# Encoder trunk: start of the FFNs, convolution module, last transposes and GLA gates of a four-layer kernel rearranged

## The chip, the cores and the metric

The kernel runs on one core of a Trainium2 chip. The metric is the device time of one execution in microseconds (us), as the median of several runs. TensorE (PE) multiplies matrices, VectorE (DVE), ScalarE (ACT) and GpSimd (POOL) work elementwise, and the queue of SyncE (SP) issues the transfers of weights.

## The reference

Four layers on `x` of 1 x 256 x 1024 (float32). Each layer is a half-step SwiGLU FFN (inner width 2816), a token mixer, and another half-step FFN, each with an RMSNorm ahead and a residual add. The mixers are, in order, dilated window attention, a Conformer convolution module, Fourier mixing and bidirectional gated linear attention (GLA). The change touches the FFN and the second and the fourth mixer:

```python
def _swiglu(h, w1, w3, w2):
    return (jax.nn.silu(h @ w1) * (h @ w3)) @ w2

def _conv_module(u, ...):
    z = u @ w_pw1 + b_pw1
    a, gate = jnp.split(z, 2, axis=-1)
    z = a * jax.nn.sigmoid(gate)
    z = lax.conv_general_dilated(z, w_dw, ...) + b_dw      # 31 taps, depthwise
    zf = (z - mu) * lax.rsqrt(var + EPS) * ln_g + ln_b     # mu, var over the 1024 features
    return jax.nn.silu(zf) @ w_pw2 + b_pw2

def _gla_direction(q, k, v, log_a, include_diag):
    # S_t = diag(a_t) S_{t-1} + k_t v_t^T, o_t = q_t S_t, in chunks of 64 tokens
...
# GLA mixer, 4 heads, q and k 512 wide, v and r 1024 wide
def log_decay(d):                                          # d: forward, backward
    z = (u @ w_a1[d]) @ w_a2[d] + b_a[d]                   # rank 16
    return jax.nn.log_sigmoid(z) / GLA_TAU
o = o_fwd + o_bwd
o = rmsnorm over each head of o, times norm_g, times silu(r)
return o @ w_o
```

## The kernel before, in words

Activations lie transposed, 128 features on the partitions by 256 tokens, in pieces `x0` to `x3`. A float32 product is made of pairs: each operand is split into a high part (rounded to fp32r) and a low part (the rest), and `mm3` issues three matmuls, high by high, high by low, low by high. All of them go through `mm` (L81). The FFN's `wide` puts two of the three into one matmul of 512 columns, so there a product is one of 256 and one of 512 columns.

Weights come in blocks of 1 MB, 128 x 2048, over SP's queue into 4 buffers `raw`. `split_block` turns a block into a pair `w`: ACT writes the high part (L167), DVE subtracts (L170). There are 4 buffers `w`; `take` hands the next pair to the matmuls in the order of a plan, `done` counts a buffer as free, and `pump(n)` emits up to `n` splits for buffers counted free. On each engine the instructions run in the order in which the code emits them, so a split stands on ACT and DVE exactly where its `pump` is in the code. PSUM has 8 banks, A0 to A3 and B0 to B3. One half collects up-projections (`ab` hands its banks out in turn) and the other half the down-projections (`dbank`); the halves change roles from stage to stage.

- **FFN** (`ffn`): blocks `w1`, `w3` in turn into banks PA, PB. ACT copies one half of the result to a tile `sl` or `br` (`parts`, L466), DVE adds the other (`add`, L471), so the banks come free. The stage begins with four k-steps of both blocks, then `pump(1)`, then the rest, since the last x come late from the stage before. `stats(True)` sums squares on PE and gives R by a Newton iteration on DVE (L410, then L367 to L373), in steps that `ffn` emits among its own. The product with the silu is split into `g` (ACT L635, DVE L636). In the last FFN, `fin_transpose` (L84) transposes the finished first half of the output on PE while the second half is multiplied.
- **Convolution** (`pre1`, `mix1`): 24 products `wd` of 128 x 256 (a mask times the taps, L671) are made on GpSimd during the FFN ahead. After the taps, the mean and variance are summed on PE, and each piece `zc` is multiplied with the inverse deviation (DVE L876), goes through Silu (ACT L880), and is split (ACT L635, DVE L636). `pump(1)` follows behind pieces 1 and 2.
- **GLA** (`pre3`, `mix3`): `qkproj` makes q and k, `qkevac` moves them out of PSUM (DVE L1223). The gate's low rank part `t1` (17 rows for each direction, one of them ones for the bias) is multiplied by `wa2` in four float32 matmuls (`gate_a`), set between steps of `qkproj(2)`. Then `vproj(i)` and `rproj(i)` (8 steps of 6 matmuls of 256 columns each) stand among the stages of the heads: `decays`, `states`, `scores`, `out` (L1403 sums squares, L1409 makes o) and `trans`, which transposes o on PE.

Of the kernel before, what the change touches and what calls it, by code (L numbers as in the profile page):

```python
# [15 lines left out]
D = 1024  # L16
# [3 lines left out]
EPS = 1e-6  # L20
NP = NG // 2
NR = 4
NW = 4
GLA_ORDER = [("gv", 0), ("gr", 0), ("gv", 1), ("gr", 1), ("gv", 2), ("gr", 2), ("gv", 3), ("gr", 3)]
# [14 lines left out]
class Enc:  # L39
    def __init__(self, ctx, tc, a, stages):  # L40
# [11 lines left out]
        self.lower, self.nab, self.held = 0, 3, []  # L52
# [9 lines left out]
    def ab(self):  # L62

        self.nab = (self.nab + 1) % 4
        while self.nab in self.held:
            self.nab = (self.nab + 1) % 4
        return self.bank(self.lower, self.nab)
# [5 lines left out]
    def bank(self, half, j):  # L73
        return self.banks[half][j]
# [25 lines left out]
    def plan(self):  # L100
# [7 lines left out]
        for st in self.stages:  # L108
# [26 lines left out]
            elif st[1] == 2:  # L135
                add(("cs",), a["c_cs"], 2)
                for j in range(4):
                    add(("wf", j), a["fnet_w"][j], 2)
            elif st[1] == 3:
                for i in range(4):  # L140
                    add(("gqk", i), a["gla_w_in"][i], 8)
                for n, i in GLA_ORDER:
                    add((n, i), a["gla_w_in"][{"gv": 4, "gr": 8}[n] + i], 8)
                for j in range(4):
                    add(("go", j), a["gla_w_o"][j], 2)
# [256 lines left out]
    def stats(self, row=False, scale=1.0):  # L402

        if row:
# [5 lines left out]
            nc.vector.tensor_scalar(y, p, 1.0 / D, EPS, ALU.mult, ALU.add)  # L410
            return self.newton_rsqrt(y, self.R, [128, 256], "nR", 1, 3)
# [31 lines left out]
    def ffn(self, l, s):  # L443
# [44 lines left out]
        for n, ks in enumerate(cuts):  # L488
            if n == len(cuts) - 1:
                if not first:  # L490
                    self.pump(1)
# [16 lines left out]
        steps.pop(0)()  # L508
        br0 = parts(PB, "br")
# [5 lines left out]
        for i in range(1, NG):  # L515
# [8 lines left out]
            if i == 4 and pre:  # L524
                self.pre = pre()
# [37 lines left out]
        for p in range(NP):  # L563
            self.pump(1)
            if p < 2 and self.nstage >= len(self.stages):
                self.fin_transpose(p)
# [79 lines left out]
    def open_pre(self):  # L646
# [3 lines left out]
        if n < len(self.stages) and self.stages[n][0] == "mix" and hasattr(self, f"pre{self.stages[n][1]}"):  # L650
            self.prest = ExitStack()
            self.prepool = self.prest.enter_context(self.tc.tile_pool(name=self.name("pre"), bufs=1))
            return getattr(self, f"pre{self.stages[n][1]}")
# [3 lines left out]
    def pre1(self):  # L657
# [9 lines left out]
        wd = {}  # L667
        for j in (0, 2, 3):
            wd[j] = self.sb(P, [128, 8, 8, 32], F32, f"wd{j}")
            for n in range(8):  # L670
                nc.gpsimd.tensor_tensor(wd[j][:, n], m32.unsqueeze(1).to_broadcast([128, 8, 32]),  # L671
                                        wt[:, 8 * j + n].unsqueeze(2).to_broadcast([128, 8, 32]), ALU.mult)
        return wc, wd

    def mix1(self):
# [102 lines left out]
        def factor():  # L778
            steps = self.stats(True)
            self.pump(1)  # L780
# [56 lines left out]
        self.sqrt_table()  # L837
        nc.vector.tensor_tensor(sqs[:, 0], sqs[:, 0], sqs[:, 1], ALU.add)
        for c in range(2):
            nc.vector.scalar_tensor_tensor(zc[3][:, c], dwp[3][:, 256 * c:256 * c + 256], self.col(("bdw", 6 + c)), m0,  # L840
                                           ALU.add, ALU.subtract)
            nc.scalar.activation(s2[:, c], zc[3][:, c], AF.Square)
        nc.vector.tensor_tensor(sqs[:, 0], sqs[:, 0], sqs[:, 2], ALU.add)
# [26 lines left out]
        nn = self.sb(ev, [128, 2, 2, 2, 256], F32R, "zs", 3)  # L870
        for i in range(4):
            gp = self.pair(self.hp, [128, 2, 256], f"x{i}") if i < 2 else nn[:, i - 2]
            hi, lo = gp[:, 0], gp[:, 1]
            for c in range(2):
                z = zc[i][:, c]
                nc.vector.tensor_tensor(z, z, rp, ALU.mult)  # L876
                gb = dict(scale=self.col(("lng", 2 * i + c)), bias=self.col(("lnb", 2 * i + c)))
                if i == 0:
                    nc.scalar.activation(hi[:, c], z, AF.Silu, **gb)
# [3 lines left out]
            if i:  # L883
                for c in range(2):
                    self.split(zc[i][:, c], gp[:, :, c])
            g.append(gp)
            if i in (1, 2):
                self.pump(1)
# [262 lines left out]
    def pre3(self):  # L1151

        nc, P = self.nc, self.prepool
        raw = lambda shape: self.sb(self.ev, shape, F32, "craw", 2)

        wa = raw([128, 8, 64])
        nc.gpsimd.memset(wa, 0.0)
        for d in range(2):
            nc.gpsimd.dma_start(wa[:, :, 32 * d:32 * d + 16],
                                self.a["gla_w_a1"][0, d].rearrange("(k p) n -> p k n", p=128))  # L1160
        traw = raw([128, 2, 256])
        nc.gpsimd.dma_start(traw, self.a["c_tri"])
        was = self.pair(P, [128, 8, 64], "was")
        self.split(wa, was)
# [3 lines left out]
        nc.gpsimd.dma_start(lraw, self.a["c_tril"])  # L1168
        mraw = raw([128, 2, 256])
        nc.gpsimd.dma_start(mraw, self.a["c_mask"])  # L1170
        lst = self.sb(P, [128, 2, 128], F32R, "lst")
        nc.scalar.activation(lst, lraw, AF.Copy)
        mask = self.sb(P, [128, 2, 256], mybir.dt.uint8, "mask")
        nc.vector.tensor_copy(mask, mraw)
        wa2 = self.sb(P, [64, 512], F32, "wa2")
        for d in range(2):
            nc.gpsimd.dma_start(wa2[32 * d:32 * d + 16, :], self.a["gla_w_a2"][0, d])
            nc.gpsimd.dma_start(wa2[32 * d + 16:32 * d + 17, :], self.a["gla_b_a"][0, d:d + 1, :])
        return was, wa2, tri, lst, mask

    def mix3(self):
# [6 lines left out]
        bkn = [0]  # L1188

        def bank(hold=False):  # L1190

            bkn[0] += 1
            if self.D4 is None and bkn[0] % 2:
                return self.dbank(bkn[0] // 2 % 4)
            p = self.ab()
            if hold:
                self.held = [self.nab]
            return p
# [7 lines left out]
        vt = [self.sb(ev, [128, 1024], F32, f"gv{t}") for t in range(2)]  # L1206
# [26 lines left out]
        for k in range(8):  # L1233
            self.mm3(pa[0:64, 0:256], was[:, :, k], self.xk(k), start=k == 0, stop=k == 7)
        self.bcast()
        t1 = T([64, 256])
        nc.gpsimd.memset(t1, 1.0)
        for d in range(2):
            pr = slice(32 * d, 32 * d + 16)
            nc.vector.tensor_tensor(t1[pr], pa[pr, 0:256], self.R[pr], ALU.mult)  # L1240
        qkevac(0, p0)
        qkevac(1, p1)

# [6 lines left out]
        def gate_a(d, t):  # L1250
            pr = slice(32 * d, 32 * d + 17)
            p = bank()
            self.mm(p, t1[pr, 128 * t:128 * t + 128], wa2[pr, :], start=True, stop=True)
# [23 lines left out]
        def vproj(i):  # L1277

            def step(k, s):
                if k == 0:  # L1280
# [291 lines left out]
def lay(a, perm=True):  # L1572


    o = {}
# [65 lines left out]
```

## Time and profile before

| | |
|---|---|
| runs, us | 1929.97, 1930.38, 1933.54 (median 1930.38) |
| the profiled execution, us | 1932.82 |
| its span, us | 1930.7 |
| PE busy | 1902.6 us (99%) in 12128 matmuls |
| PE loading weights | 1674.7 us (87%) |
| DVE busy | 1396.7 us (72%) |
| ACT busy | 994.8 us (52%) |
| POOL busy | 34.9 us (2%) |
| DMA | 338.08 MB, mean 175 GB/s |

Busy time of an engine is its share of the span; a stall of PE is told in brackets behind a row of the timeline, with the instruction that ended it.

### The profile page before, as it was taken

Reading aid. Unit: us, or ns where it says so; the run is one execution under the profiler, and the core shown is the slowest. Engines: PE = TensorE matmul, PEld = TensorE weight load, DVE = VectorE, ACT = ScalarE, POOL = GpSimd, SP = SyncE. Lnnn points to the kernel's source line nnn. Section 1 sums busy time; section 2 is a strip of 40 time slices with the busy share of each in tenths; the row PEclk is TensorE's granted clock in tenths of the full one; section 3 lists DMA queues with packets and bytes.
Section 4 is the critical chain, followed back from the end, with each engine's and each line's share of the span. In section 5 each row is a group of like instructions: output and inputs, shape, how many; then the busy total and the mean of one; then the engine's idle time right before and its main releaser. Section 6 shows DMA issues by size and latency. Waiting matters only on the chain.

```text
span 1930.7 us, 28911 instructions
## 1 busy us (share of the span) xinstructions
PE 1902.6 (99%) x12128; PEld 1674.7 (87%) x12128; DVE 1396.7 (72%) x1850; ACT 994.8 (52%) x1267; POOL 34.9 (2%) x55
## 2 busy tenths in 40 slices
PE   8999999999999999899999999999999999999998
PEld 6888899888888898788888889988888888998886
DVE  7776567877697767787768776787777766668774
ACT  6554444654455544565545554555445445756452
POOL 0000000000040000000000000000000000000000
PEclk9999999999999999899999999999999999999999
DMA  7655533465445543246545554365546553335550
GB/s 265 221 193 195 189 130 132 155 219 193 175 173 210 188 170 137 85 159 220 192 175 198 195 178 172 131 218 191 182 168 221 199 193 115 129 129 196 198 195 22
DMA packets 48643, 338.08 MB, mean 175 GB/s; under 512 B 5568, under 2 KB 5744, under 8 KB 8192
## 3 DMA queue, kind: packets, MB, share of 16 engines
q1 hardware_dynamic: 47952, 335.11, 48.8%
q8 instruction: 95, 1.56, 0.3%
q0 software_dynamic: 560, 1.12, 0.2%
q14 instruction: 36, 0.29, 0.0%
HBM read 335.16 MB, written 1.05 MB: 174 GB/s over the span
## 4 chain that ended last, share of the span: by engine, by line
PE 92%; DVE 5%; ACT 2%; issue 1%; DMA 0%; SPq 0%; DVEq 0%; ACTq 0%
PE B L81 50%; PE A L81 41%; DVE w L170 1%; ACT w L167 1%; DVE zc L765 1%; PE A L84 0%; DMA h<-in_x_dram 0%; ACT zc L880 0%; ACT x L302 0%; PE B L84 0%; DVE h L279 0%; DVE acc L355 0%; DVE x L304 0%; DVE sl L474 0%; DVE nRu L372 0%
## 5 line engine op out<-in xcount | busy, mean ns | idle before, releaser
L170 DVE TENSOR_TENSOR w<-raw,w 128x2048 fp32r<-128x2048 f32 x315 | 720.2, 2293 | 288.6 <-ACT w L167 288.2
L167 ACT ACTIVATE w<-raw 128x2048 fp32r<-128x2048 f32 x315 | 598.9, 1909 | 113.5 <-PE A L81 47.4
L81 PE MATMUL B<-x,w 128*128 128x256 f32 (+1 forms) x3968 | 643.7, 322 | 1.3 <-DVE sl L471 1.1
L81 PEld LDWEIGHTS B<-x,w 128*128 128x128 f32 x3968 | 571.3, 190 | 71.5 <-issue 5.5
L81 PE MATMUL A<-x,w 128*128 128x256 f32 x3008 | 521.5, 334 | 10.3 <-DVE w L636 6.8
L81 PEld LDWEIGHTS A<-x,w 128*128 128x128 f32 x3008 | 455.8, 190 | 73.1 <-DVE w L636 6.8
L81 PE MATMUL B<-g,w 128*128 128x256 f32 (+1 forms) x1408 | 251.2, 336 | 0.7 <-DVE w L170 0.6
L81 PE MATMUL A<-g,w 128*128 128x256 f32 (+1 forms) x1408 | 250.3, 336 | 0.0
L81 PEld LDWEIGHTS B<-g,w 128*128 128x128 f32 x1408 | 216.5, 187 | 32.7 <-issue 0.9
L81 PEld LDWEIGHTS A<-g,w 128*128 128x128 f32 x1408 | 216.6, 187 | 31.5
L635 ACT ACTIVATE g<-br 128x512 fp32r<-128x512 f32 x88 | 55.6, 632 | 253.6 <-DVE br L480 253.6
L474 DVE TENSOR_TENSOR sl<-sl,R 128x512 f32<-128x512 f32 x176 | 121.7, 695 | 2.5
L636 DVE TENSOR_TENSOR g<-br,g 128x512 fp32r<-128x512 f32 x88 | 61.1, 695 | 61.5 <-ACT g L635 61.5
L302 ACT ACTIVATE x<-h,cols 128x256 fp32r<-128x256 f32 x88 | 39.9, 501 | 67.8 <-DVE h L279 49.0
L466 ACT ACTIVATE br<-B 128x256 f32<-128x256 f32 x88 | 30.2, 385 | 75.0 <-PE B L81 75.0
L477 ACT ACTIVATE sl<-sl 128x512 f32<-128x512 f32 x88 | 55.0, 628 | 26.6 <-DVE sl L474 26.5
L466 ACT ACTIVATE br<-A 128x256 f32<-128x256 f32 x88 | 30.1, 384 | 70.4 <-PE A L81 70.4
L480 DVE TENSOR_TENSOR br<-sl,br 128x512 f32<-128x512 f32 x88 | 60.6, 689 | 0.5
L81 PE MATMUL B<-w,x 128*128 128x256 f32 (+2 forms) x360 | 60.8, 327 | 0.0
L81 PEld LDWEIGHTS B<-w,x 128*128 128x128 f32 x360 | 53.4, 190 | 5.9 <-issue 0.3
L466 ACT ACTIVATE sl<-A 128x256 f32<-128x256 f32 x88 | 29.8, 377 | 52.6 <-PE A L81 52.6
L466 ACT ACTIVATE sl<-B 128x256 f32<-128x256 f32 x88 | 29.9, 377 | 49.6 <-PE B L81 49.2
(293 smaller groups left out, 1085.1 us busy)
## 6 DMA issues: line engine op xcount, KB each, us to landing
raw<-in_ffn_w_dram SPq DMA_DIRECT2D x262, 1024.0 KB, 4.8
raw<-in_attn_w_qk_dram SPq DMA_DIRECT2D x12, 1024.0 KB, 4.7
raw<-in_conv_w_pw_dram SPq DMA_DIRECT2D x12, 1024.0 KB, 4.8
raw<-in_gla_w_in_dram SPq DMA_DIRECT2D x12, 1024.0 KB, 4.7
raw<-in_attn_w_v_dram SPq DMA_DIRECT2D x6, 1024.0 KB, 4.8
raw<-in_fnet_w_dram SPq DMA_DIRECT2D x4, 1024.0 KB, 4.9
raw<-in_gla_w_o_dram SPq DMA_DIRECT2D x4, 1024.0 KB, 4.8
raw<-in_ffn_w_dram SPq DMA_DIRECT2D x8, 256.0 KB, 6.3
```

The source lines that it names most:

```text
L81: return self.nc.tensor.matmul(out, lhsT, rhs, start=start, stop=stop, skip_group_check=True)
L167: self.nc.scalar.activation(w[:, 0], raw, AF.Copy)
L170: (eng or self.nc.vector).tensor_tensor(w[:, 1], raw, f32(w[:, 0]), ALU.subtract)
L302: nc.scalar.activation(xh[:, c], h[:, c], AF.Copy, scale=g[c])
L466: nc.scalar.activation(t[:, c], P[c][:, 1], AF.Copy)
L474: nc.vector.tensor_tensor(t, t, self.Rb(), ALU.mult)
L477: nc.scalar.activation(t, t, AF.Silu)
L480: nc.vector.tensor_tensor(br, sl, br, ALU.mult)
L635: self.nc.scalar.activation(p[:, 0], src, AF.Copy)
L636: self.nc.vector.tensor_tensor(p[:, 1], src, f32(p[:, 0]), ALU.subtract)
L765: nc.vector.scalar_tensor_tensor(o, x, w, o, ALU.mult, ALU.add)
```

## The change

1. `ffn` emits its second `pump` later (`pump(self.pend - 1)` instead of `pump(1)` there), and `stats` hands the first Newton instruction out as a step too, so that both adds into `sl` come ahead of it.
2. `pre1` and `pre3` become generators. `ffn` takes one step at `w1` blocks 4, 6 and 8 and two at each of the last five down steps; the 24 products are on VectorE, three to a step.
3. In `mix1`, the multiplications with the inverse deviation (`scaled`) of pieces 1, 2 and 3 come ahead of the pumped splits, and piece 3's subtraction and squares ahead of a table load.
4. `fin_transpose(0)` and `(1)` move from down steps 0 and 1 to 3 and 4.
5. In GLA the weights of v and r are stacked: `vrproj(i)` has 8 steps of 6 matmuls of 512 columns into two banks. The gate's part is held as an fp32r stack of high and low rows, 64 partitions a direction, and a gate is two fp32r matmuls (64 and 32 rows). `ab` hands out the bank taken longest ago, at first over both halves, and the fills among the head stages are other.

```diff
@@ ab, let_go
+        b = min((self.taken[i][j], i != self.lower, i, j) for i in range(2) for j in range(4)
+                if (both or i == self.lower) and (i, j) not in self.held)[2:]
...
@@ stats
-            nc.vector.tensor_scalar(y, p, 1.0 / D, EPS, ALU.mult, ALU.add)
-            return self.newton_rsqrt(y, self.R, [128, 256], "nR", 1, 3)
+            steps = []
+            def begin():
+                nc.vector.tensor_scalar(y, p, 1.0 / D, EPS, ALU.mult, ALU.add)
+                steps.extend(self.newton_rsqrt(y, self.R, [128, 256], "nR", 1, 3))
+            steps.append(begin)
+            return steps
@@ ffn
                 if not first:
-                    self.pump(1)
+                    self.pump(self.pend - 1)
                 up(wa, PA, ks[:2])
...
         steps.pop(0)()
+        steps.pop(0)()
         br0 = parts(PB, "br")
...
-            if i == 4 and pre:
-                self.pre = pre()
+            if i in PRE_AT and pre:
+                next(pre, None)
...
             self.pump(1)
-            if p < 2 and self.nstage >= len(self.stages):
-                self.fin_transpose(p)
+            if pre:
+                next(pre, None)
+                next(pre, None)
+            if p > 2 and self.nstage >= len(self.stages):
+                self.fin_transpose(p - 3)
@@ pre1
+        for j in wd:
             for n in range(8):
-                nc.gpsimd.tensor_tensor(wd[j][:, n], m32.unsqueeze(1).to_broadcast([128, 8, 32]),
+                if n % 3 == 0:
+                    yield
+                nc.vector.tensor_tensor(wd[j][:, n], m32.unsqueeze(1).to_broadcast([128, 8, 32]),
@@ mix1
+        def scaled(i):
+            for c in range(2):
+                z = zc[i][:, c]
+                nc.vector.tensor_tensor(z, z, rp, ALU.mult)
...
-            if i:
+            if i == 0:
+                scaled(1)
+                scaled(2)
+            else:
                 for c in range(2):
                     self.split(zc[i][:, c], gp[:, :, c])
             g.append(gp)
+            if i == 1:
+                scaled(3)
             if i in (1, 2):
                 self.pump(1)
@@ mix3
-            self.mm3(pa[0:64, 0:256], was[:, :, k], self.xk(k), start=k == 0, stop=k == 7)
+            self.mm3(pa[:, 0:256], was[:, :, k], self.xk(k), start=k == 0, stop=k == 7)
...
-            nc.vector.tensor_tensor(t1[pr], pa[pr, 0:256], self.R[pr], ALU.mult)
+            nc.gpsimd.memset(t1[64 * d:64 * d + 1], 1.0)
+        nc.scalar.activation(t2, t1, AF.Copy)
+        for d in range(2):
+            pr = slice(64 * d + 32, 64 * d + 64)
+            nc.vector.tensor_tensor(t2[pr], t1[pr], f32(t2[pr]), ALU.subtract)
...
-            self.mm(p, t1[pr, 128 * t:128 * t + 128], wa2[pr, :], start=True, stop=True)
+            for n in range(2):
+                pr = slice(64 * d, 64 * d + (64, 32)[n])
+                self.mm(p, t2[pr, 128 * t:128 * t + 128], wa2[pr, n], start=n == 0, stop=n == 1)
...
+                    for n, (a, b) in enumerate(((0, 0), (0, 1), (1, 0))):
+                        self.mm(p[t], x[:, a], w[:, b, k % 4], start=k == 0 and n == 0, stop=k == 7 and n == 2)
...
+        for hd in range(4):
             decays, states, scores, out, trans = H[hd]
+            early[0] = hd < 3
             decays()
             self.pump()
...
+                f = vrproj(hd + 1)
+                n = (4, 2, 2)
             else:
...
+                n = (10, 8, 6)
+            fill(f, n[0])
+            states()
+            if 0 < hd < 3:
+                H[hd - 1][4]()
+            fill(f, n[1])
+            scores()
+            if hd == 3:
+                H[2][4]()
             self.pump()
-            fill(f, 4)
+            fill(f, n[2])
             out()
         fill(f)
         H[3][4]()
```

VectorE at the start of the FFN ahead of the convolution, first before, then of the change (`x3` is the last piece that the matmuls wait for, `w` a weight pair, `R` and `nR` the Newton iteration, A0 to A3 the banks PA and PB, `sl` and `br` their results):

```order
474 L304 SCALAR_TENSOR_TENSOR x3_410_4542<-sl_406_4527,cols_79,x3_410_4542 128x256 x2
475 L170 TENSOR_TENSOR w_413_4586<-raw_396_4368,w_413_4586 128x2048
476 L410 TENSOR_SCALAR R_415_4599<-B0_73 128x256
477 L367 TENSOR_SCALAR nRu_418_4605<-R_415_4599 128x256
478 L368 TENSOR_SCALAR R_416_4600<-nRu_418_4605 128x256
479 L471 TENSOR_TENSOR sl_419_4616<-sl_419_4616,A0_69 128x256
480 L471 TENSOR_TENSOR sl_419_4616<-sl_419_4616,A1_70 128x256
```

```order
474 L315 SCALAR_TENSOR_TENSOR x3_410_4542<-sl_406_4527,cols_79,x3_410_4542 128x256 x2
475 L488 TENSOR_TENSOR sl_415_4606<-sl_415_4606,A0_69 128x256
476 L488 TENSOR_TENSOR sl_415_4606<-sl_415_4606,A1_70 128x256
477 L424 TENSOR_SCALAR R_413_4594<-B0_73 128x256
478 L378 TENSOR_SCALAR nRu_417_4629<-R_413_4594 128x256
...
486 L488 TENSOR_TENSOR br_418_4635<-br_418_4635,A2_71 128x256
487 L488 TENSOR_TENSOR br_418_4635<-br_418_4635,A3_72 128x256
488 L181 TENSOR_TENSOR w_419_4643<-raw_396_4368,w_419_4643 128x2048
```

The split (row 475 before) stands behind both pairs of adds now (row 488), and the Newton iteration between them.

VectorE at the end of the convolution, before and of the change (`zc1` to `zc3` times the inverse deviation in a bank B, then the low parts into `x1` and `zs`):

```order
692 L876 TENSOR_TENSOR zc1_535_6077<-zc1_535_6077,B0_73 128x256 x2
693 L636 TENSOR_TENSOR x1_576_6992<-zc1_535_6077,x1_576_6992 128x256 x2
694 L170 TENSOR_TENSOR w_577_7001<-raw_550_6268,w_577_7001 128x2048
695 L876 TENSOR_TENSOR zc2_566_6831<-zc2_566_6831,B0_73 128x256 x2
696 L636 TENSOR_TENSOR zs_574_6982<-zc2_566_6831,zs_574_6982 128x256 x2
697 L170 TENSOR_TENSOR w_579_7014<-raw_554_6350,w_579_7014 128x2048
698 L876 TENSOR_TENSOR zc3_569_6942<-zc3_569_6942,B0_73 128x256 x2
```

```order
699 L897 TENSOR_TENSOR zc1_535_6077<-zc1_535_6077,B2_75 128x256 x2
700 L897 TENSOR_TENSOR zc2_566_6831<-zc2_566_6831,B2_75 128x256 x2
701 L657 TENSOR_TENSOR x1_576_6996<-zc1_535_6077,x1_576_6996 128x256 x2
702 L897 TENSOR_TENSOR zc3_569_6942<-zc3_569_6942,B2_75 128x256 x2
703 L181 TENSOR_TENSOR w_577_7005<-raw_550_6268,w_577_7005 128x2048
704 L657 TENSOR_TENSOR zs_574_6982<-zc2_566_6831,zs_574_6982 128x256 x2
705 L181 TENSOR_TENSOR w_579_7016<-raw_554_6350,w_579_7016 128x2048
```

All three multiplications stand ahead of both splits now; before, a split stood ahead of each of the last two.

The four gates on TensorE, before and of the change (`wa2` the gate's weights, the rows of 6 steps of `qkproj(2)`):

```order
7882 L81 MATMUL A0_69<-wa2_1019_12673,t_1104_13841 128x512
7883 L81 MATMUL B0_73<-x2_1087_13646,w_1085_13620 128x256 x6
7884 L81 MATMUL B1_74<-wa2_1019_12673,t_1104_13841 128x512
7885 L81 MATMUL B0_73<-x3_1089_13674,w_1085_13620 128x256 x6
7886 L81 MATMUL A1_70<-wa2_1019_12673,t_1104_13841 128x512
7887 L81 MATMUL B0_73<-x3_1089_13674,w_1085_13620 128x256 x6
7888 L81 MATMUL B2_75<-wa2_1019_12673,t_1104_13841 128x512
```

```order
7882 L91 MATMUL A2_71<-wa2_1074_13464,t2_1105_13842 128x512 x2
7883 L91 MATMUL B3_76<-x2_1089_13648,w_1087_13622 128x256 x6
7884 L91 MATMUL A3_72<-wa2_1074_13464,t2_1105_13842 128x512 x2
7885 L91 MATMUL B3_76<-x3_1091_13676,w_1087_13622 128x256 x6
7886 L91 MATMUL B0_73<-wa2_1074_13464,t2_1105_13842 128x512 x2
7887 L91 MATMUL B3_76<-x3_1091_13676,w_1087_13622 128x256 x6
7888 L91 MATMUL B1_74<-wa2_1074_13464,t2_1105_13842 128x512 x2
```

The places are the same, with other banks and two matmuls in place of one. VectorE there, before and of the change (`t` and `t2` the gate's part, `qT` the evacuation of q):

```order
1394 L1240 TENSOR_TENSOR t_1104_13841<-B3_76,R_1103_13839 16x256 x2
1395 L1223 SCALAR_TENSOR_TENSOR qT_1095_13693<-B1_74,R_1103_13839 128x512
1396 L170 TENSOR_TENSOR w_1105_13846<-raw_1082_13549,w_1105_13846 128x2048
1397 L170 TENSOR_TENSOR w_1107_13851<-raw_1084_13586,w_1107_13851 128x2048
1398 L1223 SCALAR_TENSOR_TENSOR qT_1095_13693<-B2_75,R_1103_13839 128x512
```

```order
1403 L1266 TENSOR_TENSOR t_1104_13841<-B2_75,R_1103_13839 128x256
1404 L1272 TENSOR_TENSOR t2_1105_13842<-t_1104_13841,t2_1105_13842 32x256 x2
1405 L1250 SCALAR_TENSOR_TENSOR qT_1097_13695<-B0_73,R_1103_13839 128x512
1406 L181 TENSOR_TENSOR w_1106_13850<-raw_1084_13551,w_1106_13850 128x2048
1407 L181 TENSOR_TENSOR w_1108_13855<-raw_1086_13588,w_1108_13855 128x2048
1408 L1250 SCALAR_TENSOR_TENSOR qT_1097_13695<-B1_74,R_1103_13839 128x512
```

The fourth gate takes the bank that the last of these rows empties, before (B2, row 1398) as of the change (B1, row 1408); two more instructions stand ahead of it.

## Rows read from the trace of the kernel before

**Rows 1.** Page, part 1: busy us (share of the span) and instructions of each engine.

```profile
PE 1902.6 (99%) x12128; PEld 1674.7 (87%) x12128; DVE 1396.7 (72%) x1850; ACT 994.8 (52%) x1267; POOL 34.9 (2%) x55
```

**Rows 2.** Waits of PE: line waiting, instruction waited for, us in total, times, longest.

```profile
PE A L84 <- DVE h L279: 1.9, 1, 1.9
```

**Rows 3.** Timeline of the last FFN's end: start, us, engine, line, shape [idle before].

```profile
1891.67 0.63 PE L84 MATMUL A<-ident,x 128*128 128x128 f32 x4 [1.91 <-DVE h L279]
1892.05 5.86 PE L81 MATMUL B<-g,w 128*128 128x256 f32 x32
```

**Rows 4.** Timeline, FFN ahead of the convolution, its start and later.

```profile
533.61 21.90 POOL L671 TENSOR_TENSOR wd<-m,wt 128x256 f32<-128x256 f32 x24 [1.39 <-DMA wt<-in_conv_w_taps_dram]
535.37 22.46 PE L81 MATMUL A<-x,w 128*128 128x256 f32 x128 [1.39 <-DVE sl L471]
535.57 0.75 DVE L371 TENSOR_TENSOR nRt<-R 128x256 f32<-128x256 f32 x1
...
558.40 6.25 PE L81 MATMUL B<-g,w 128*128 128x256 f32 x32 [0.58 <-DVE w L170]
...
642.47 5.76 PE L81 MATMUL B<-g,w 128*128 128x256 f32 x32
```

**Rows 5.** Timeline, start of an FFN behind an FFN with POOL idle.

```profile
1016.92 0.42 DVE L371 TENSOR_TENSOR nRt<-R 128x256 f32<-128x256 f32 x1
1021.47 2.29 DVE L170 TENSOR_TENSOR w<-raw,w 128x2048 fp32r<-128x2048 f32 x1
```

**Rows 6.** Timeline, start of the FFN behind the attention.

```profile
349.45 8.88 PE L81 MATMUL B<-x,w 128*128 128x256 f32 x48 [0.95 <-DVE sl L471]
352.94 2.28 DVE L170 TENSOR_TENSOR w<-raw,w 128x2048 fp32r<-128x2048 f32 x1
```

**Rows 7.** Timeline, end of the convolution.

```profile
799.68 2.29 DVE L170 TENSOR_TENSOR w<-raw,w 128x2048 fp32r<-128x2048 f32 x1 [1.35 <-ACT w L167]
...
809.99 10.68 PE L81 MATMUL A<-zs,w 128*128 128x256 f32 x84 [1.62 <-ACT zs L635]
```

**Rows 8.** Windows, end of the convolution and GLA's gates; PEclk is the granted clock.

```profile
755.00:800.00 45.00, 41.04 (x537) 31.28 (x536) 32.03 (x77) 19.10 (x42) 0.00 (x0) 0.89 0.07 25
1615.00:1635.00 20.00, 20.00 (x111) 15.60 (x110) 11.09 (x14) 16.65 (x22) 0.00 (x0) 0.83 0.27 107
```

**Rows 9.** Chain that ended last: 36 matmuls of 512 columns; 48 of 256.

```profile
196.03 8.18 PE B L81 x36
...
1634.89 5.76 PE A L81 x48
```

**Rows 10.** Timeline, GLA's gates.

```profile
1618.92 1.12 PE L81 MATMUL A<-wa,t 17*128 17x512 f32 x2
...
1620.88 1.12 PE L81 MATMUL B<-wa,t 17*128 17x512 f32 x2
...
1622.13 0.68 DVE L1223 SCALAR_TENSOR_TENSOR qT<-B,R 128x512 f32<-128x512 f32 x1
```

**Rows 11.** Timeline, PE in a head's states.

```profile
1685.57 0.48 PE L81 MATMUL B<-gv,ks 64*128 64x256 f32 x1
1685.89 0.38 PE L81 MATMUL B<-gv,ks 64*128 64x256 f32 x1
1686.11 0.38 PE L81 MATMUL B<-gv,ks 64*128 64x256 f32 x1
```

**Rows 12.** Timeline, ACT in a head of GLA.

```profile
1694.40 0.84 ACT L1290 ACTIVATE gv<-A,rc 128x256 f32<-128x256 f32 x2 [2.62 <-PE A L81]
1697.58 1.28 ACT L1351 ACT_TABLE_LOAD   x1
```

**Rows 13.** Timeline, the last head's end.

```profile
1710.44 10.13 PE L81 MATMUL A<-og,w 128*128 128x256 f32 x84
...
1715.17 0.88 DVE L1409 SCALAR_TENSOR_TENSOR t<-B,ro,rg 128x256 f32<-128x256 f32 x2
1720.40 0.60 PE L84 MATMUL B<-ident,t 128*128 128x128 f32 x4
```

## What I predict, blind

> **What bounds the kernel now.** I read the page's busy shares first: PE is busy for 1902.6 of 1930.7 us [rows 1], so the time is PE's work, its clock and its few stalls. Nothing is gained by relieving an engine as such; each part of the change is worth what it takes from one of these three. I then listed PE's waits, with the longest of those that the change touches in [rows 2], and went to each in the timeline to see what ends it and what stands around it. The windows of the stretches around the second and fourth mixer show where the granted clock is not full [rows 8], and the chain that ended last gives the pace of unstalled matmuls by width [rows 9]. A wait's bracket is not its whole price: behind a stall the first matmuls come slower, so where I can I compare the run of matmuls with one of the same kind that was not disturbed.
>
> **Last transposes.** The first transposes in the last FFN stand ahead of the matmuls of the next block and wait 1.91 us for DVE, which has just finished the half that they take; the 32 matmuls behind them need 5.86 us [rows 3] where 32 of the same kind need 5.76 us [rows 4]. Three steps later their operand is long there. What comes after them in PE's order, the same matmuls, has its weights split by then. Gain 1.91 + 0.10 = 2.0 us.
>
> **Weight products.** The 24 products keep GpSimd busy for 21.90 us from 533.61 us, and in that stretch a Newton multiplication on DVE takes 0.75 us [rows 4] where it takes 0.42 us at another FFN's start, with GpSimd idle [rows 5]. DVE's additions into `sl` and a split come late by it: PE waits 1.39 us and 0.58 us, and the 32 matmuls behind the second wait need 6.25 us instead of 5.76 us [rows 4]. Without GpSimd beside it, DVE keeps the pace of the other FFNs, which have neither wait. The 24 products then cost DVE about 24 x 0.42 = 10 us, an estimate from a multiplication of the same size [rows 5], in pieces of three over one FFN; DVE is busy 72% of the time [rows 1], and PE has no wait for it in the FFN's inner loops, so I cost them at nothing. If this cover were gone, a piece of three would delay a split by 1.3 us. Gain 1.39 + 0.58 + 0.49 = 2.45 us.
>
> **Start of the FFNs.** Behind an FFN, the split that moves behind the Newton steps would be done about where the one at 1021.47 us now begins [rows 5], and its block is wanted a little later, by my count of the steps about half a microsecond; so nothing is gained or lost. Behind the attention PE waits 0.95 us for `sl`, since a split stood ahead [rows 6]. That wait goes, but DVE works without a break from there to the end of the split at 352.94 + 2.28 = 355.2 us, and PE wants that split's result by then: the wait moves there. The same holds behind GLA. I take 0; from below it may lose 1 us in each of two places, from above win 0.95 us.
>
> **End of the convolution.** The last piece's split waits behind two weight splits on DVE, of which one takes 2.29 us; PE waits 1.62 us for it, and its next 84 matmuls need 10.68 us [rows 7] where 84 x 0.120 = 10.08 us would do at the pace of [rows 9] (5.76/48). With the multiplications ahead of the splits, ACT gets the last piece about 5 us earlier. Gain 1.62 + 0.60 = 2.2 us. The clock's fall in this stretch, granted 0.89 on the mean [rows 8], comes from the waits of the norm's chain ahead of it, which stays; I count nothing for it. Piece 3's squares ahead of a table load shorten that chain by some tenths, and I leave them out.
>
> **GLA, v and r.** 384 matmuls of 256 columns become 192 of 512. [Rows 9] give 5.76/48 = 0.120 us for one and 8.18/36 = 0.227 us for the other: 46.1 - 43.6 = 2.5 us gained. The Trainium skill, in "TensorE: Matmul & The Clock Gate" under "Wait — 56ns, not 53.3ns?", has a fixed cost of about 2.5 ns for each matmul at full clock beside its columns. By that, an estimate from the page, the halved count would be worth only about 0.5 us; the 256-column pace of this trace is further above its columns than that, so the page and the rows differ, and the rows decide.
>
> **GLA, gates.** The gates follow each other at 1620.88 - 1618.92 = 1.96 us [rows 10]; six matmuls of 256 columns between them take 6 x 0.12 = 0.72 us, so a gate costs 1.24 us. Two matmuls of 512 columns cost at least 2 x 0.227 = 0.45 us and, as they change the rows of the array used, a little more: where the states' 64-row matmuls begin, the first step is 0.32 us and the next 0.22 us [rows 11], so 0.1 us for a change. With three changes I take 0.75 us (0.45 to 1.24 the bounds). Gain 4 x 0.49 = 2.0 us. The Trainium skill, "TensorEngine Tiling (Array Packing)" under "Key Properties", says that a change of tiling mode drains TensorE. That speaks against a 64-row matmul followed by a 32-row one, and the trace agrees in kind, at 0.1 us a change; at a full gate's 1.24 us the gain here would be nothing.
>
> **GLA, clock.** In the window of the gates the granted clock is 0.83 [rows 8], that is (1 - 0.83) x 20 / 0.5 = 6.8 us at the lower level, 1.2 GHz, which cost 3.4 us. The engine did the 64-column low rank part and the 17-row gates before it fell; both are replaced by full-width ones. I take it that it does not fall; the bounds are 0 and 3.4 us.
>
> **GLA, new waits.** The fourth gate writes the bank that DVE's last row of the gates' stretch empties, behind two weight splits; that began at 1622.13 us and took 0.68 us [rows 10]. It will be later by about 1.7 us, an estimate: four more steps of the kind that take 0.84/2 = 0.42 us [rows 12] make the gate's part, ahead of it in DVE's order. So it ends at 1624.5 us, and PE would be there at 1618.92 + 3 x 1.47 = 1623.3 us; with a restart 1.3 us of wait (0 to 2.1). `out` of the first head can wait for its operands behind two splits, 0.6 us (0 to 2.3). After the last `out`, 84 matmuls (10.13 us) stood ahead of the last transposes, whose operand was there at 1715.17 + 0.88 = 1716.05 us, 5.6 us after these 84 began [rows 13]. Of them 24 are left, 24 x 0.12 = 2.9 us; the squares, the Newton steps and the product take about 4.4 us when no split is between. Wait 1.5 us (0 to 2.7). Together 3.4 us. So GLA gives 2.5 + 2.0 + 3.4 - 3.4 = 4.5 us.
>
> **Sum.** 2.0 + 2.45 + 0 + 2.2 + 4.5 = 11.1 us off the profiled execution's 1932.82 us: 1921.7 us. It lay 2.44 us above the median of 1930.38 us, so the median should be 1919.2 us, its own range 1916.5 to 1921.5 us.
>
> **Rivals.**
> - The clock falls in GLA as before: the narrow matmuls may not be its reason, since in the convolution it falls in a stretch with waits [rows 8]. The new wait of the fourth gate lies in the same place. 1919.2 + 3.4 = 1922.6 us.
> - The new waits in GLA do not appear, because splits are rarer in ACT's and DVE's order than I counted: 1919.2 - 3.4 = 1915.8 us.
> - The fixed cost per matmul as the skill has it, which gives 2.0 us less for v and r: 1921.2 us. For it speaks that [rows 9] come from two stages, against it that no other cost is seen between them.
> - The stalls removed ahead of and in the convolution come back beside their places, as I expect behind the attention [rows 6], because the chain on DVE is what really bounds there: 2.45 + 2.2 = 4.65 us less gain, 1923.9 us; and with the clock's fall too 1927.3 us.
> - Slower: ACT becomes the bound in GLA. Each stacked group ends in four evacuations at once, 4 x 0.42 us, and the two kinds (copies and silus) ask for a table load each, 1.28 us [rows 12]: 4.2 us in one piece, held by two banks. If PE came to the first matmul that needs them before that is over, each head would lose up to 4.2 us, four heads 17 us: 1936 us. It decides at whether 4 steps, 24 x 0.227 = 5.4 us, cover it; by these rows they do, unless a weight split stands between as well.
>
> **How the numbers follow.** Chances: forecast 0.50, clock 0.15, no new waits 0.15, fixed cost 0.04, stalls come back 0.12 (0.07 alone, 0.05 with the clock), ACT 0.04. The predicted time is that of the likeliest. The range from 1914.5 us (no new waits, with the upper bounds at the FFNs' starts) to 1925.5 us (stalls back, with a loss there) leaves out the last two cases and the tails of the others, some 0.2 in all. A measurement of this kernel can tell about 0.2%, 3.9 us, from no change: 1927.3 us is within it, 1923.9 us not. So faster 0.91, same 0.05, slower 0.04.
>
> **What would show it.** Right: no wait of PE for `h` at L84 in the last FFN, none for `sl` in the FFN ahead of the convolution, Newton multiplications at 0.42 us there, no wait for `zs` at the convolution's end, 1.0 granted in the gates' window, and v and r at 0.227 us a matmul. Waits of about 1 us each at the fourth gate and ahead of the last transposes, and one of about 1 us behind the attention 5 us later than now. Wrong: a granted clock under 0.9 in the gates' window; waits of PE for ACT in the heads; a wait for the first piece of `wd`; or matmuls of v and r above 0.24 us.

## The result and the profile after

The changed kernel takes 1921.99 us (median of four runs, 1921.67 to 1922.22), beside 1931.96 us for the kernel before on the same chip: a ratio of 0.9944, 95% interval 0.9932 to 0.9956. That is 10.0 us less, where 11.1 us were forecast, and 2.8 us above the predicted time.

From one sum of squares on PE to the next, the profiled executions took, in us (the second column is a second profile of the kernel before, told of below):

| stretch | before | before, again | after | difference to the first |
|---|---|---|---|---|
| start up to the FFN ahead of the convolution | 529.36 | 530.02 | 529.36 | 0.0 |
| FFN ahead of the convolution | 187.28 | 187.25 | 184.67 | -2.6 |
| convolution | 110.93 | 111.76 | 106.95 | -4.0 |
| the next four stages (FFN, FFN, Fourier mixing, FFN) | 594.82 | 594.55 | 594.30 | -0.5 |
| FFN ahead of GLA | 183.67 | 184.10 | 185.73 | +2.1 |
| GLA | 133.47 | 133.49 | 130.51 | -3.0 |
| last FFN | 182.52 | 182.28 | 180.27 | -2.3 |
| rest | 8.64 | 8.64 | 8.62 | 0.0 |

In the four stages behind the convolution its FFN gave 0.7 us and the next one lost 0.2 us; no run was made to say why.

The page's first part, which answers to [rows 1]:

```profile
PE 1895.0 (99%) x11936; PEld 1662.2 (87%) x11936; DVE 1401.6 (73%) x1877; ACT 999.2 (52%) x1272; POOL 10.7 (1%) x28
```

PE's waits, the rows that are new or moved. The wait for `h` of [rows 2] is gone, and so are those for `zs` and `sl`; in their place stand waits in GLA (`S`, `t`, `P`, `qT`), ahead of it (`x`), and behind the attention and GLA (`w`):

```profile
PE B L91 <- DVE w L181: 1.5, 2, 1.0
...
PE B L91 <- DVE S L1403: 1.0, 1, 1.0
PE B L94 <- DVE t L1435: 0.9, 1, 0.9
...
PE B L91 <- DVE x L315: 0.7, 2, 0.4
PE B L91 <- ACT x L313: 0.4, 1, 0.4
...
PE A L91 <- DVE P L1414: 0.2, 1, 0.2
PE B L91 <- DVE qT L1250: 0.2, 1, 0.2
```

Timeline of the places of [rows 3], [rows 4] and [rows 7]. The Newton steps take 0.42 us instead of 0.75, the 32 matmuls 5.77 us, the last two pieces' 96 matmuls run in one piece, and the transposes have no bracket:

```profile
533.61 0.42 DVE L383 SCALAR_TENSOR_TENSOR nRu<-nRt,R 128x256 f32<-128x256 f32 x1
...
556.49 5.77 PE L91 MATMUL B<-g,w 128*128 128x256 f32 x32
...
802.52 11.68 PE L91 MATMUL A<-zs,w 128*128 128x256 f32 x96
...
1898.26 0.60 PE L94 MATMUL A<-ident,x 128*128 128x128 f32 x4
```

Windows of the stretches of [rows 8] (the second a little wider), the granted clock behind the five busy times: 0.92 instead of 0.89, and 1.00 at the gates.

```profile
755.00:800.00 45.00, 41.02 (x550) 32.01 (x550) 35.86 (x83) 22.86 (x48) 0.00 (x0) 0.92 0.07 21
1605.00:1635.00 30.00, 29.84 (x192) 25.75 (x191) 17.87 (x21) 19.78 (x25) 0.61 (x2) 1.00 0.32 115
```

Timeline of the end of the FFN ahead of GLA, where the time was lost. ACT waits 9.14 us for the transfer of `tri`, issued when the step before had freed the one buffer `craw`; three splits bunch up behind (DVE until 1593.78 us), the close of `h` begins 1 us after PE has come to the new `x`, and PE waits three times:

```profile
1573.55 0.54 POOL L1200 DMA_DIRECT2D craw<-in_c_tri_dram  x1 [46.84 <-DVE wa L657]
1579.99 0.63 ACT L1203 ACTIVATE tri<-craw 128x512 fp32r<-128x512 f32 x1 [9.14 <-DMA craw<-in_c_tri_dram]
...
1587.08 6.69 DVE L181 TENSOR_TENSOR w<-raw,w 128x2048 fp32r<-128x2048 f32 x3
...
1592.71 3.14 PE L91 MATMUL B<-x,w 128*128 128x256 f32 x25
1593.69 1.41 DVE L290 SCALAR_TENSOR_TENSOR h<-A,h 128x256 f32<-128x256 f32 x4
...
1596.15 1.57 PE L91 MATMUL B<-x,w 128*128 128x256 f32 x11 [0.30 <-DVE x L315]
...
1598.08 0.38 PE L91 MATMUL B<-x,w 128*128 128x256 f32 x1 [0.36 <-ACT x L313]
...
1598.87 2.30 PE L91 MATMUL B<-x,w 128*128 128x256 f32 x17 [0.40 <-DVE x L315]
```

Timeline of the gates, beside [rows 10]: they follow each other at 1615.63 - 1613.88 = 1.75 us, 0.21 us less than before, and the fourth waits 0.16 us:

```profile
1613.88 0.93 PE L91 MATMUL A<-wa,t 64*128 64x512 f32 x2
...
1615.63 0.93 PE L91 MATMUL A<-wa,t 64*128 64x512 f32 x2
...
1619.39 0.92 PE L91 MATMUL B<-wa,t 64*128 64x512 f32 x2 [0.16 <-DVE qT L1250]
```

Timeline of the last head, beside [rows 13]. A weight split stands on DVE ahead of the evacuation of the states (L1403), and `scores` waits for their bank; the last transposes wait for o, with 24 matmuls ahead of them:

```profile
1698.57 2.28 DVE L181 TENSOR_TENSOR w<-raw,w 128x2048 fp32r<-128x2048 f32 x1
1700.77 1.65 DVE L1403 SCALAR_TENSOR_TENSOR S<-S,dc,B 128x256 f32<-128x256 f32 x4
...
1702.17 1.13 PE L91 MATMUL B<-E,Em 128*128 128x128 f32 x8 [1.03 <-DVE S L1403]
...
1708.09 3.11 PE L91 MATMUL A<-og,w 128*128 128x256 f32 x24
...
1712.07 0.94 PE L94 MATMUL B<-ident,t 128*128 128x128 f32 x4 [0.87 <-DVE t L1435]
```

And the chain that ended last, v's and r's matmuls of 512 columns: 2.27/10 = 0.227 us, the pace of [rows 9].

```profile
1659.92 2.27 PE A L91 x10
```

### The profile page after: what moved, and what is told of

Same layout as the page of the kernel before. It is cut to its first block, busy times and chain, and to the rows that moved or that the text cites. A ratio compares the mean times of both kernels' runs of the same rounds, so it can differ in the third digit from the quotient of the medians.

```text
span 1920.4 us, 28519 instructions
## 1 busy us (share of the span) xinstructions
PE 1895.0 (99%) x11936; PEld 1662.2 (87%) x11936; DVE 1401.6 (73%) x1877; ACT 999.2 (52%) x1272; POOL 10.7 (1%) x28
## 4 chain that ended last, share of the span: by engine, by line
PE 90%; DVE 5%; ACT 2%; issue 1%; DMA 0%; SPq 0%; DVEq 0%; POOL 0%; POOLq 0%; ACTq 0%
PE B L91 47%; PE A L91 42%; DVE w L181 1%; ACT w L178 1%; DVE zc L787 1%; PE A L94 0%; DMA h<-in_x_dram 0%; DVE x L315 0%; ACT x L313 0%; DVE h L292 0%; DVE acc L366 0%; PE B L94 0%; DVE h L290 0%; SPq L225 0%; DVE s L1097 0%
## 5 line engine op out<-in xcount | busy, mean ns | idle before, releaser
L91 PE MATMUL B<-w,x 128*128 128x512 f32 (+1 forms) x216 | 50.0, 379 | 0.0
L488 DVE TENSOR_TENSOR sl<-sl,A 128x256 f32<-128x256 f32 x88 | 33.1, 416 | 21.8 <-ACT sl L483 21.8
```

Source lines behind the costliest of these rows:

```text
L91: return self.nc.tensor.matmul(out, lhsT, rhs, start=start, stop=stop, skip_group_check=True)
L488: nc.vector.tensor_tensor(t[:, c], t[:, c], P[c][:, 0], ALU.add)
```

## The experiments

All but the kernel before, again, start from the changed kernel. The medians come from three chips and are compared loosely; the stretches of the profiled executions, as in the table above, carry the verdicts, one trace each. Where nothing in a stretch was edited, the traces differ by 0.5 us in the FFN ahead of the convolution (184.15 to 184.67 us), by 1.0 us in the convolution (106.70 to 107.67 us), by 0.1 us in GLA and 0.3 us in the last FFN.

**Products back on GpSimd.**

```diff
-                nc.vector.tensor_tensor(wd[j][:, n], m32...
+                nc.gpsimd.tensor_tensor(wd[j][:, n], m32...
```

> The changed kernel with the 24 products back on GpSimd, all else as changed. My theory, that GpSimd's products slow VectorE beside them and so make the FFN's first additions and splits late, expects a Newton multiplication of about 0.75 us there, waits of PE of 1 to 2 us in the first 25 us of that FFN, and 1923.0 to 1924.5 us. The rival, that the new order of the additions ahead of the Newton iteration cured these waits, expects no wait there and 1922.0 us.

Measured 1925.35 us (five runs, 1925.23 to 1926.29). The FFN takes 188.31 us, 3.6 more than with the change and 1.0 more than before. Its timeline shows Newton steps at 0.72 us, and waits for two splits:

```profile
535.22 0.72 DVE L382 TENSOR_TENSOR nRt<-R 128x256 f32<-128x256 f32 x1
...
540.71 16.92 PE L91 MATMUL A<-x,w 128*128 128x256 f32 x96 [1.03 <-DVE w L181]
...
558.82 1.98 PE L91 MATMUL B<-g,w 128*128 128x256 f32 x9 [1.18 <-DVE w L181]
```

My theory holds in kind, and its price was too low: besides the two waits there is a third of 0.34 us, and the time lies 0.85 us above the expected range. With GpSimd at work beside it the new order alone makes the FFN worse.

**Old order at the FFNs' starts.** `pump(1)` again ahead of the additions, and Newton's first steps ahead of them:

```diff
-                    self.pump(self.pend - 1)
+                    self.pump(1)
...
         sl0 = parts(PA, "sl")
+        if not first:
+            steps.pop(0)()
         add(sl0, PA)
```

> The changed kernel with the old order at the start of every FFN (a split ahead of the additions, Newton's first steps ahead of them). My theory, that the order is worth nothing in total, expects 1921.5 to 1922.5 us, no wait ahead of the convolution, and behind the attention a wait of about 1 us for the additions at about 349 us in place of the one for a split at about 355 us. The rival, that the order gave a part of the 2.6 us gained ahead of the convolution, expects 1923 to 1924.5 us.

Measured 1923.46 us (1922.01 to 1924.78). Behind the attention the wait stands at 349 us again and the stretch is the same (186.22 us beside 186.35). But the FFN ahead of the convolution takes 185.58 us, 0.9 more than with the change, whose 184.67 us is the longest of the traces with nothing edited there, with the wait for `sl` though Newton's steps take 0.42 us:

```profile
535.35 9.99 PE L91 MATMUL A<-x,w 128*128 128x256 f32 x56 [1.02 <-DVE sl L488]
535.55 0.42 DVE L382 TENSOR_TENSOR nRt<-R 128x256 f32<-128x256 f32 x1
```

So here the rival is right: the order is worth about 1 us, and nothing elsewhere.

**The norm's multiplications back behind the splits; the table load back; both.** In the first, `scaled` goes and each piece is multiplied in its own turn; in the second, `sqrt_table()` and one addition stand ahead of piece 3 again.

> The changed kernel with the norm's multiplications back behind the pumped splits. My theory, that the wait for the last piece's split is removed by them alone and the shorter stretch at the lower clock is not, expects a wait of about 1.6 us for the last piece, 6.8 us at the lower clock as in the changed kernel, and 1924.2 us. The rival, that the shorter stretch comes from them as well, expects 10.2 us at the lower clock and 1925.9 us.

> The changed kernel with the convolution's table load back ahead of the third piece's subtraction and squares. My theory, that this move shortens the chain ahead of the norm and with it the stretch at the lower clock, expects 10.2 us at the lower clock and 1923.7 to 1924.0 us. The rival, that the stretch became shorter for another reason, expects 6.8 us at the lower clock and 1922.0 to 1922.4 us.

> The changed kernel with both edits at the convolution's end undone (norm's multiplications behind the splits and the table load ahead of the third piece). Each alone left 6.8 us at the lower clock. If the two together shortened it, 10.2 us at the lower clock come back here and the stretch from the sum of squares ahead of the convolution to that of the next FFN takes 110.5 to 111 us, as before; if the stretch's length has another reason, 6.8 us stay and it takes 109 to 110 us.

The first: 1926.21 us (six runs, 1923.11 to 1927.86); its profiled execution, the fastest of them, has the wait (1.43 us for `zs`), a convolution of 109.82 us, 6.8 us at the lower clock, and 1.00 granted behind the wait:

```profile
805.38 10.68 PE L91 MATMUL A<-zs,w 128*128 128x256 f32 x84 [1.43 <-ACT zs L656]
```

By this trace the theory holds; the median lies 2.0 us above its time and close to the rival's, and no slower execution was traced. The second: 1922.77 us, a convolution of 107.81 us, 6.8 us at the lower clock. Here the rival is right: the table load does not set that length, and its move is worth next to nothing. Both: one run, 1926.88 us; a wait of 1.8 us, a convolution of 111.82 us, and 10.2 us at the lower clock, but in two pieces, 6.8 us ahead of the wait and 3.4 us behind it, which neither reading expected (windows, 0.83 granted):

```profile
806.00:816.00 10.00, 9.56 (x65) 9.37 (x66) 7.94 (x11) 6.41 (x10) 0.00 (x0) 0.83 0.65 252
```

The second fall stands also in the second profile of the kernel before, here in its windows and timeline:

```profile
806.00:816.00 10.00, 7.43 (x49) 7.05 (x49) 7.29 (x7) 5.51 (x7) 0.00 (x0) 0.83 0.40 135
```

```profile
810.34 11.90 PE L81 MATMUL A<-zs,w 128*128 128x256 f32 x84 [2.57 <-ACT zs L635]
```

**The kernel before, again.**

> The kernel before, unchanged, for a second look at its stretches at the lower clock. If these belong to the program, they are again 10.2 us at the convolution's end and 6.8 us at GLA's gates. If they depend on something that differs between executions, one or both have another length or are missing.

One run, 1934.22 us, with 10.2 us at the lower clock in the convolution again, but now 6.8 us ahead of the wait for `zs` and (1 - 0.83) x 10 / 0.5 = 3.4 us behind it, where the first profile had them in one piece ahead of it. At GLA's gates it has 6.8 us again. So the fall at `zs` differs between executions: of four traces with the wait two have it there, one has a longer fall ahead, and one has neither; of ten without the wait none has more than 6.8 us in the stretch.

**First transposes back at steps 0 and 1.**

> The changed kernel with the first two transposes of the last FFN back at down steps 0 and 1. My theory, that their wait was the whole effect, expects a wait of 1.9 us for h and 1924.0 us. The rival, that the matmuls behind would have waited for their weights anyway, expects 1922.0 to 1922.5 us.

Measured 1922.64 us (1921.98 to 1923.86). The last FFN takes 182.04 us, 1.8 more. The wait is split in two, and shorter than the 1.91 us of [rows 3]:

```profile
1881.49 0.51 PE L94 MATMUL A<-ident,x 128*128 128x128 f32 x2 [0.32 <-ACT x L321]
1882.66 0.44 PE L94 MATMUL A<-ident,x 128*128 128x128 f32 x2 [0.67 <-DVE h L290]
```

By the stretch the theory's sum holds, but not its wait: 0.99 us of 1.8 us stand in brackets. The median alone lies by the rival's range; the profiled execution, 1923.26 us, had no loss ahead of GLA (below), which hides 1.8 us.

**One step of GLA's preparation at each down step.**

```diff
                 next(pre, None)
-                next(pre, None)
+                if pre.__name__ == "pre1":
+                    next(pre, None)
```

> The changed kernel, but in the FFN ahead of GLA one step of the preparation at each of the last five down steps instead of two. My theory, that two steps at once make ScalarE wait 9 us for a transfer issued one step earlier, so that splits bunch up and the last closes of the FFN come late, expects that wait to go, with it the three waits for x at 1595 to 1599 us (1.65 us with what is slow behind them), and 1920.0 us. The rival, that these waits come from the larger stack of gate weights or the later weight transfers, expects them to stay and 1922.0 us.

Measured 1920.72 us (1920.13 to 1921.58). The FFN ahead of GLA takes 183.89 us, 1.8 less; ACT still waits for `tri`, but a split stands ahead of that wait, and PE's waits for `x` are gone:

```profile
1577.71 0.63 ACT L1204 ACTIVATE tri<-craw 128x512 fp32r<-128x512 f32 x1 [5.64 <-DMA craw<-in_c_tri_dram]
...
1590.88 1.41 DVE L290 SCALAR_TENSOR_TENSOR h<-A,h 128x256 f32<-128x256 f32 x4
...
1592.13 6.63 PE L91 MATMUL B<-x,w 128*128 128x256 f32 x54
```

This trace alone does not settle it, because its transfer was also a quick one (issued at 1572.97 us, used at 1577.71 us: 4.7 us). Of nine traces with two steps at once, six took 185.4 to 185.8 us there, with 6.0 to 6.5 us from issue to use, and three 184.0 to 184.2 us, with 4.5 to 4.7 us. All three with one step took 183.9 us, and in one of them, the version without the gates at the end of this section, the transfer took 6.6 us; a split stands ahead of it, and PE has no wait:

```profile
1575.13 0.54 POOL L1201 DMA_DIRECT2D craw<-in_c_tri_dram  x1 [46.84 <-DVE wa L658]
1581.75 0.63 ACT L1204 ACTIVATE tri<-craw 128x512 fp32r<-128x512 f32 x1 [7.52 <-DMA craw<-in_c_tri_dram]
...
1594.29 6.62 PE L91 MATMUL B<-x,w 128*128 128x256 f32 x54
```

So with two steps the loss hangs on how long a transfer takes, and with one step a slow transfer costs nothing there. The rival is out: the larger stack of gate weights is in all twelve traces, the waits in six. What makes one transfer slower than another was not looked into.

**Last head's split behind the states, other fills.**

```diff
             decays()
-            self.pump()
             if hd < 3:
+                self.pump()
...
-                n = (10, 8, 6)
+                n = (10, 6, 5)
             fill(f, n[0])
             states()
+            if hd == 3:
+                self.pump()
```

> The changed kernel, but in the last head of GLA the weight split behind the states instead of ahead of them, and the fills 10, 6, 5 instead of 10, 8, 6, so that 11 steps stay for the end. My theory, that a split on VectorE ahead of the evacuation of the states' banks makes scores wait (1.2 us), and that too few steps are left ahead of the last transposes (1.2 us), expects both waits to go and 1919.6 to 1920.5 us. The rival, that the time is bound by the chain on ScalarE and VectorE behind it up to the next FFN, expects a wait of the same size further on and 1921.5 to 1922.0 us.

Measured 1919.37 us (1919.01 to 1921.15). GLA takes 128.38 us, 2.1 less. The theory holds: the states are evacuated ahead of the split, the transposes have 33 matmuls ahead of them, and neither has a wait:

```profile
1697.87 1.65 DVE L1403 SCALAR_TENSOR_TENSOR S<-S,dc,B 128x256 f32<-128x256 f32 x4
1699.55 2.29 DVE L181 TENSOR_TENSOR w<-raw,w 128x2048 fp32r<-128x2048 f32 x1
1699.57 1.05 PE L91 MATMUL B<-E,Em 128*128 128x128 f32 x8
...
1705.25 4.14 PE L91 MATMUL A<-og,w 128*128 128x256 f32 x33
```

**Gates of 128 rows.** `t2` is held for each direction with the other's rows zero:

```diff
-                pr = slice(64 * d, 64 * d + (64, 32)[n])
-                self.mm(p, t2[pr, 128 * t:128 * t + 128], wa2[pr, n], start=...
+                self.mm(p, t2[:, d, 128 * t:128 * t + 128], wa2[:, n], start=...
```

> The changed kernel, but with all 128 rows in each gate matmul (the gate's part is held twice, with the rows of the other direction zero). My theory, that the price of a gate (0.86 us instead of 2 x 0.23 us) is the change of the rows used, 0.2 us at each matmul, expects 0.23 to 0.26 us for each of the eight matmuls, 1.5 us less at the gates, less what the longer chain to the gate's part makes the first or the fourth gate wait (up to 0.5 us): 1920.5 to 1921.0 us. The rival, that a first fp32r matmul of 512 columns behind others costs 0.4 us by itself, expects 0.4 us for each and 1922.0 us.

Measured 1923.79 us (1921.83 to 1924.24), slower than expected. The price was right: a gate's two matmuls cost no more than others of 512 columns, and gates follow each other at 1615.60 - 1614.43 = 1.17 us instead of 1.75. But the fourth now comes before its bank is free, waits 2.12 us, and the clock falls behind the wait (windows: 0.66 granted, 3.4 us at the lower level):

```profile
1614.43 0.62 PE L91 MATMUL A<-wa,t 128*128 128x512 f32 x2
...
1615.60 0.63 PE L91 MATMUL A<-wa,t 128*128 128x512 f32 x2
...
1620.25 1.04 PE L91 MATMUL B<-wa,t 128*128 128x512 f32 x2 [2.12 <-DVE qT L1250]
```

```profile
1620.00:1625.00 5.00, 4.75 (x25) 4.55 (x26) 0.39 (x2) 4.91 (x8) 0.00 (x0) 0.66 0.80 336
```

**All three, and q's second half evacuated ahead of the two splits (`qkevac(0, p0, False)`); the same without the gates.**

> The changed kernel with three edits at once: one step of GLA's preparation at each down step, the last head's split behind the states with fills 10, 6, 5, and gates of 128 rows, and besides q's second half evacuated ahead of the two weight splits, so that the fourth gate's bank is free in time. By my theory the three are in different places and add up: 2.1 + 2.1 us as the traces of the two apart showed, and at the gates 8 x (0.43 - 0.23) = 1.6 us, without the 2.1 us wait and the low clock that the gates alone brought: 1916 to 1917 us. The rival, that the work on VectorE only moves and a split comes late at the next weights in GLA, expects 1918 us or more and a wait for a split within 15 us behind the gates.

> The same without the gates of 128 rows: q's second half ahead of the splits, one step of the preparation at each down step, the last head's split behind the states. Theory: 1917.5 to 1918.5 us, no wait at the fourth gate (0.2 us in the changed kernel). Rival as for the version with the gates: 1919 us or more.

1916.38 us (1915.76 to 1916.81) and 1918.44 us (1917.74 to 1919.87), beside 1931.88 us before on the same chip: ratios 0.9921 (0.9907 to 0.9934) and 0.9932 (0.9920 to 0.9945). GLA takes 125.84 and 128.14 us. Both times lie in their expected ranges. With all three the fourth gate has no wait, 1.00 is granted there, and the gains add up; this version is 15.5 us faster than the kernel before, where the change gave 10.0 us.

```profile
1615.53 0.63 PE L91 MATMUL B<-wa,t 128*128 128x512 f32 x2
```

```profile
1600.00:1630.00 30.00, 30.00 (x213) 28.17 (x213) 17.43 (x31) 20.23 (x25) 0.61 (x2) 1.00 0.29 106
```

## Why the prediction was right, and where not

That the sum came out near is in part luck: the convolution gave 1.8 us more than forecast, while GLA gave 1.5 us less and the FFN ahead of it lost 2.1 us that no term had. The sum missed the profiled execution by 0.5 us (1922.22 us beside 1921.7 us). The rest of the 2.8 us is the last step, which took off 2.44 us because the profiled execution lay that far above its median; of the changed kernel it lies 0.23 us above.

**Last transposes**, 2.0 us forecast: 2.3 us in the stretch, 1.8 us by undoing them. Right.

**Weight products**, 2.45 us: the FFN won 2.6 us. But the step "DVE keeps the pace of the other FFNs, which have neither wait" was half wrong: with the old order the wait for `sl` stays at 1.02 us with GpSimd idle, and [rows 6] had such a wait of 0.95 us in another FFN. Products alone give 187.28 - 185.58 = 1.7 us, the order alone loses 1.0 us, both together win 2.6 us. **Start of the FFNs**, 0, was right behind the attention (the wait went to 355 us, 1.03 us) and nearly so behind GLA (0.19 us of wait became 0.50), and wrong ahead of the convolution, where the order is worth 0.9 us once the products are on DVE.

**End of the convolution**, 2.2 us: 4.0 us. The wait was sized rightly: bringing it back cost 2.1 to 3.1 us with no fall behind it (109.82 us beside 106.70 to 107.67 us). The step that failed is "I count nothing for it" on the clock: 3.4 us less at the lower level gave 1.7 us. A second fall at the wait for `zs` is seen in two of four traces that have the wait and in none without; that the wait brings it is not shown, and why the first profile had all 10.2 us ahead of the wait stays open.

**v and r**, 2.5 us: the 384 matmuls of before stand for 46.96 us up to their successors' starts, the 192 for 44.97, so 2.0 us; most of them stand at the 0.120 and 0.227 us forecast, and the missing 0.5 us lies at the places where other matmuls follow (0.3 us and more in place of 0.227) and at the wait of `out`. The fixed cost, as the Trainium skill ("TensorE: Matmul & The Clock Gate", "Wait — 56ns, not 53.3ns?") has it, would have given 0.5 us, an estimate from its 2.5 ns for each matmul; the trace does not agree.

**Gates**, 2.0 us: 4 x 0.21 = 0.8 us. Mis-sized was "0.1 us for a change" of rows. With 128 rows throughout, a gate's period falls by 0.58 us, on the mean 0.19 us for each of three changes, twice my price; part of it falls on the 128-row matmuls beside the gates (0.21 and 0.22 us in place of 0.12), which I had left at 0.12 us each. The Trainium skill ("TensorEngine Tiling (Array Packing)", "Key Properties") says that a change of tiling mode drains TensorE; the trace agrees in kind.

**Clock at the gates**, 3.4 us: 1.00 granted, and 6.8 us at the lower level in both traces of before. The number is right; the reason is only argued. The new gates have 64 and 32 rows, so they are not "full-width", and no run puts back the low rank part or the gates by themselves.

**New waits in GLA**, 3.4 us: their brackets hold 2.3 us, and the other terms leave 3.2 us of the stretch for them with what is slow behind them; but they are not where I put them. The fourth gate waited 0.16 us, as PE came later than I had it (a gate takes 1.03 us in place of 0.75) and only one more instruction stands ahead of it on DVE, not two; `out` of the first head 0.23 us; the last transposes 0.87 us; and `scores` of the last head, which I had not named, 1.03 us.

**FFN ahead of GLA**: no term of the sum, and 2.1 us lost. The step that is missing is the price of `pre3`'s waits on transfers in ACT's order, put at nothing without a reason: with one step at a time the loss is gone even where the transfer took 6.6 us. I gave two steps at each down step no thought, though they stand in the diff.

## What to carry to other kernels

When preparation is spread over a loop on an engine that runs in order, count from each transfer's issue to its use: a step that consumes what the step just ahead has issued stops everything behind it. When a bank or buffer is freed sooner or later, look at what stands ahead of the instruction that frees it; a 2.3 us split there decided two of the waits. And a wait can come dearer than its bracket: at the end of three of them the clock fell for 3.4 us, which is 1.7 us more.

## What was not expected of the hardware

At the end of a stall of PE of 1.8 to 2.6 us, or within 1.6 us behind it, 3.4 us at the lower clock began in three traces (before again, both edits undone, gates of 128 rows); behind one of 1.43 us, the 1.62 us of [rows 7] and the 1.91 us of [rows 3] no fall came, so its length alone doesn't tell. Going from 128 rows of the array to 64, to 32 and back cost 0.58 us, on the mean 0.19 us a change; that the change costs it, and not the smaller number of rows itself, is seen only for the 128-row matmuls at either side.
